# Down projection of a hybrid attention layer: ten and thirteen pairs by seven products, the first one's sums queued further on, the first half's closing additions in steps

## The chip, the cores and the metric

The kernel runs on one core of one Trainium2 chip. A core has several engines that each work through their own list of instructions in order and wait for one another by semaphores: TensorE (PE in the profile: matrix products; PEld is its loading of weights), VectorE (DVE), ScalarE (ACT), GpSimd (POOL) and SyncE (SP). SP, ACT and POOL also issue DMA transfers, each from a queue of its own (SPq, POOLq). The metric is device time in microseconds (us), the median of several runs.

## What is computed

One decoder layer on 256 positions with 2048 channels, in float32: a combined input projection, two kinds of attention side by side (8 heads each), an output projection, and an MLP of 8192 hidden channels. The change lies in the last step, the product of `u` (256 x 8192) with `w_down` (8192 x 2048) and the norm around it:

```python
x = x + _rmsnorm(mixed @ w_out[layer], norm_attn_post[layer])
h = _rmsnorm(x, norm_mlp_pre[layer])
u = jnp.square(jax.nn.relu(h @ w_up[layer]))
x = x + _rmsnorm(u @ w_down[layer], norm_mlp_post[layer])
```

## The kernel before

**Float32 by two parts.** Every operand of a product is split into two float32r parts: ACT copies it to `hi` (line 307) and DVE subtracts to get `lo` (line 308). A product is then three matmuls, hi·hi, hi·lo and lo·hi, all issued by the helper at line 297. The same is done for the weights, tile by tile, as they come from memory.

**The down projection** runs in two halves of the output's columns, c = 0 (columns 0 to 1023) and c = 1 (1024 to 2047). Each half sums over 64 chunks of 128 hidden channels, taken as 32 pairs. Four PSUM banks per half hold the result `y`: two blocks of positions (b) by two column groups of 512 (n). A pair is worked in one of two ways:

- As two single chunks ("k" steps): each chunk is one weight tile of 128 x 1024, multiplied into four banks by three matmuls each, 24 matmuls for the pair.
- By seven products ("w" step, a Strassen scheme): the pair and the two blocks of positions form a 2 x 2 by 2 x 2 block product, done with seven block products in place of eight. Seven times three is 21 matmuls. Four of the products go into banks `md1`, `md6`, `md7`, `md5`, apart from `y`. In exchange DVE has to form sums: of the weights (tiles `t` and `u`, in `st_down`, lines 360 to 365), giving four weight tiles to split in place of two (called b11, b, u, t below; b11 is half as wide), and of the activations (`four_sums`, lines 1028 to 1030, then split into the tile `s`). The tuple `DOWN_SEVEN` lists which pairs of each half go this way.

For pairs that are in both halves' lists (`SHARED`), the parts `s` formed in half 0 are stored to memory by `keep_s` (SP, line 1022) and fetched again in half 1 by `down_back` (POOL, line 407), so that half 1 doesn't form them anew. The lo parts of `u` are likewise stored and fetched (`ukeep`, lines 1018 and 1011), one for each group of two pairs.

**Closing a half.** When the last pair by seven products of a half is through, `close` (lines 1085 and 1088) combines the md banks into four correction tiles. When all pairs are through, half 0 is finished by `half_evac` (lines 1217 to 1227), while half 1 has begun: for each of its four banks DVE adds the correction to `y` (line 1223), ACT takes the sum of squares (`square`, line 1165), and DVE multiplies by the norm's gain (line 1227). The md banks of half 1 are the y banks of half 0, so half 1's first pair by seven products cannot start before `half_evac` has read them.

**The order of the work** is written by the program itself. All weight tiles of the program form one list (`weights.specs`). When PE is about to use tile i, `weights.get` emits the loads and splits up to tile i + 6 (`W_AHEAD`). The tiles lie in 8 slots (`W_BUFS`) and a slot is rewritten only when PE has used its tile; the loaded raw tiles lie in 5 (`RAW_BUFS`). `plan_seven` hangs the sums of a pair by seven products on a place in this list: `SUMS_AHEAD` = 2 tiles ahead of the pair's first tile, with the activations' sums two and one places before that. The load of the pair's weights goes on POOL's queue, into `ab_down` or, in turn, into `c` (half 0) or into `uT0` and `uT1` (half 1); as every engine's list is in order, POOL issues it as soon as the buffer's last readers are done. Chains such as `half_evac` are Python generators; each `yield` gives a time, in planned microseconds, after which the next piece is written into the engines' lists.

The tiles `s` have two buffers, `uhi`/`ulo` (the split `u` of a group of two pairs) also two.

Of the kernel before, what the change touches and what calls it, by code (L numbers as in the profile page):

```python
# [23 lines left out]
OP = mybir.AluOpType  # L24
# [5 lines left out]
NB = S // P  # L30
# [66 lines left out]
SUMS_AHEAD, LOAD_AHEAD = 2, 3  # L97
# [15 lines left out]
D_PREP = (50.0, 24.0, 12.0)  # L113


DOWN_SEVEN = ((7, 11, 13, 17, 19, 23, 25, 29), (4, 7, *range(9, 28, 2)))
SHARED = [k for k in DOWN_SEVEN[0] if k in DOWN_SEVEN[1]]
GT = FF // 512
DOWN_STEPS = [[s for kp in range(2 * GT)
# [145 lines left out]
def layer(nc, tc, io):  # L265
# [52 lines left out]
    weights = Weights(nc, wp, split, W_BUFS, W_AHEAD)  # L318
# [87 lines left out]
        st, left[c, kp] = down_parts(c, kp)  # L406
        nc.gpsimd.dma_start(out=st.bitcast(F32), in_=skeep[kp])

    def plan_seven(sums, fs, early, after, more=(), last=(), soon=False):

        at = max(len(weights.specs) - SUMS_AHEAD, after)
        if soon:
            more = (*more, (at - max(at - LOAD_AHEAD, after - 2), early))
        for n, f in (*more, (0, sums), *((0, f) for f in last)):
            weights.first.setdefault(at - n, []).append(f)
        return [weights.plan(f) for f in fs], len(weights.specs)
# [3 lines left out]
    wide_u, after, after_p = [], 0, 0  # L420
    for j in range(NUP):
        wide_u.append([])
        for what, k in UP_STEPS[j]:
            if what == "k":
                g = () if k in SCALED.get(j, ()) else (gcol[:, 8 + k:9 + k],)
                ts = [weights.plan(up_weight(j, k), 1, CW, *g)]
            elif what == "p":
# [3 lines left out]
                if j < 5:  # L431
                    at = max(len(weights.specs) - 2 * LOAD_AHEAD, after_p)
                    weights.first.setdefault(at, []).append(
                        lambda kept=kept: nc.gpsimd.dma_start(out=late["tu"], in_=kept))
                    ts = [weights.plan(src, 1, n) for src, n in srcs[:2]] + [weights.plan(
                        lambda hi, lo, o=o: split(hi, lo, late["tu"][:, o:o + CW])) for o in (CW, 0)]
                    after_p = len(weights.specs)
                else:
                    ts = [weights.plan(src, 1, n) for src, n in srcs]
            else:  # L440
                ts, after = plan_seven(*seven_up(j, k), after, soon=j < NUP - 1 or k == 0)
# [5 lines left out]
    def seven_down(c, kp):  # L447
        def load():

            n = DOWN_SEVEN[c].index(kp)  # L450
            raw = dpl["ab"]
            if n % 2:
                raw = [uT[i].rearrange("p k s -> p (k s)") for i in range(2)] if c else late["c"]
            return load_two(raw, nc.gpsimd, io["w_down"][2 * kp * P:(2 * kp + 2) * P, c * CW:(c + 1) * CW])

        return seven(load, lambda: [late["st"][:, i * CW:(i + 1) * CW] for i in range(2)])

    dpl, left, skeep, wide_d = {}, {}, {}, []
    for c in range(2):
        wide_d.append([])  # L460
        for what, k in DOWN_STEPS[c]:
            if what == "k":
                ts = [weights.plan(down_weight(c, k), 1, CW)]
            else:
                q, parts_q, back = [lambda c=c, k=k, f=f: f(c, k) for f in (down_sums, down_split, down_back)]
                more = ((), (back,)) if c and k in SHARED else (((2, q), (1, parts_q)),)
                ts, after = plan_seven(*seven_down(c, k), after, *more)
            wide_d[c].append((what, k, ts))

    def in_order(n, apart=(0, 0)):  # L470
# [392 lines left out]
    parts = [0] * NB  # L863
# [80 lines left out]
    for ns in ((0, 1), (2,), (3,)):  # L944
# [4 lines left out]
        for c, b, acc in proj(mixT, [ch_o[n] for n in ns], f"o{ns[0]}", order, heads_done):  # L949
            n = ns[c]  # L950
# [81 lines left out]
    sums = []  # L1032
# [130 lines left out]
    def square(n, b):  # L1163
        junk = dpl["dp"].tile([P, 512], BF16, tag="junk", bufs=1, name=f"junkd{n}{b}")
        nc.scalar.activation(junk, y[b][n], AF.Square, accum_out=ssd[b][:, n:n + 1])
# [51 lines left out]

    def half_evac(more, g_half):

        for n in range(2):  # L1220
            for b in range(NB):
                tt, out = nc.vector.tensor_tensor, more[b, n]
                tt(out=y[b][n], in0=y[b][n], in1=out, op=OP.add)
                yield 1.0
                square(n, b)
                yg[n, b] = out
                tt(out=out, in0=y[b][n], in1=g_half[n], op=OP.mult)
                yield 1.0

    def three_more(out, a, w):  # L1230

# [127 lines left out]
```

## Time and profile before

| what | before |
|---|---|
| three runs | 1047.55, 1047.61, 1047.78 us (median 1047.61) |
| the profiled execution | 1047.46 us, of which the span of the profile is 1045.7 us |
| TensorE clock granted, mean | 0.998 |
| PE busy | 1036.0 us, 4841 matmuls |
| DVE busy | 807.4 us, 1077 instructions |
| ACT busy | 636.5 us |
| DMA | 260.81 MB, mean 249 GB/s |
| the down projection, first matmul to end of the span | 700.89 to 1045.7 us |

How to read the rows that follow. A row of a group gives line, engine, operation, output tile <- inputs, shapes and count, then busy us in total and the mean in ns of one. A row of the timeline begins with start and duration in us, counted from the start of the span; in square brackets is the idle time just before it and what ended it. Consecutive instructions of an engine overlap a little: a DVE subtraction of 128 x 1024 lasts 1.22 us, yet the next one starts 1.14 us after it.

### The profile page before, as it was taken

Reading aid. Unit: us, or ns where it says so; the run is one execution under the profiler, and the core shown is the slowest. Engines: PE = TensorE matmul, PEld = TensorE weight load, DVE = VectorE, ACT = ScalarE, POOL = GpSimd, SP = SyncE. Lnnn points to the kernel's source line nnn. Section 1 sums busy time; section 2 is a strip of 40 time slices with the busy share of each in tenths; the row PEclk is TensorE's granted clock in tenths of the full one; section 3 lists DMA queues with packets and bytes.
Section 4 is the critical chain, followed back from the end, with each engine's and each line's share of the span. In section 5 each row is a group of like instructions: output and inputs, shape, how many; then the busy total and the mean of one; then the engine's idle time right before and its main releaser. Section 6 shows DMA issues by size and latency. Waiting matters only on the chain.

```text
span 1045.7 us, 13573 instructions
## 1 busy us (share of the span) xinstructions
PE 1036.0 (99%) x4841; PEld 862.9 (83%) x4841; DVE 807.4 (77%) x1077; ACT 636.5 (61%) x855; POOL 99.5 (10%) x157
## 2 busy tenths in 40 slices
PE   9999999999999999999999999999999999999996
PEld 6888889888888888888888888888888888888885
DVE  7666536567557659988889798887899988989995
ACT  7675436566545558666756766665666564766662
POOL 0011111112001000010100000000000001112100
PEclk9999999999999999999999999999999999999999
DMA  9999879699878296757766656468778767789952
GB/s 340 344 304 277 216 204 318 201 252 302 235 215 262 86 352 210 263 207 246 259 207 231 222 198 213 148 231 312 256 271 314 261 226 262 263 301 323 364 195 83
DMA packets 93141, 260.81 MB, mean 249 GB/s; under 512 B 8721, under 2 KB 12817, under 8 KB 91665
## 3 DMA queue, kind: packets, MB, share of 16 engines
q1 hardware_dynamic: 71056, 190.09, 52.6%
q0 software_dynamic: 21152, 68.69, 23.2%
q10 hardware_dynamic: 864, 1.16, 0.3%
q8 instruction: 38, 0.62, 0.2%
q14 instruction: 31, 0.25, 0.1%
HBM read 244.18 MB, written 39.32 MB: 271 GB/s over the span
## 4 chain that ended last, share of the span: by engine, by line
PE 98%; DMA 1%; DVE 0%; ACT 0%; SPq 0%; DVEq 0%; POOL 0%; issue 0%; ACTq 0%
PE y L297 26%; PE acc_u L297 25%; PE acc_o L297 8%; PE m L297 7%; PE md L297 5%; PE acc_v L297 4%; PE acc_qk L297 4%; PE acc_ckv L297 2%; PE acc_ukv L297 2%; PE acc_q L297 2%; PE acc_cq L297 2%; PE acc_k L297 2%; PE acc_uq L297 2%; PE rt L301 1%; PE y L1233 1%; PE sc_b L297 1%
## 5 line engine op out<-in xcount | busy, mean ns | idle before, releaser
L308 DVE TENSOR_TENSOR lo<-raw,hi 128x1024 fp32r<-128x1024 f32 (+3 forms) x240 | 269.2, 1139 | 95.1 <-ACT hi L307 94.2
L307 ACT ACTIVATE hi<-raw 128x1024 fp32r<-128x1024 f32 (+3 forms) x240 | 234.4, 990 | 96.6 <-DMA raw<-in_w_in 20.7
L297 PE MATMUL y<-hi,uhi 128*128 128x512 f32 x376 | 146.7, 390 | 0.0
L297 PE MATMUL y<-hi,ulo 128*128 128x512 f32 x376 | 146.3, 389 | 0.0
L297 PE MATMUL y<-lo,uhi 128*128 128x512 f32 x376 | 146.3, 389 | 0.0
L297 PE MATMUL acc_u<-hi,hT_hi 128*128 128x512 f32 x356 | 141.6, 398 | 0.0
L297 PE MATMUL acc_u<-hi,hT_lo 128*128 128x512 f32 x356 | 139.1, 391 | 0.0
L297 PE MATMUL acc_u<-lo,hT_hi 128*128 128x512 f32 x356 | 138.9, 390 | 0.0
L312 DVE SCALAR_TENSOR_TENSOR lo<-raw,gcol,hi 128x1024 fp32r<-128x1024 f32 x72 | 90.6, 1280 | 18.0 <-ACT hi L311 17.7
L311 ACT ACTIVATE hi<-raw,gcol 128x1024 fp32r<-128x1024 f32 x72 | 81.9, 1149 | 21.0 <-DMA raw<-in_w_up 12.9
L297 PEld LDWEIGHTS y<-hi,ulo 128*128 128x128 f32 x376 | 70.6, 188 | 14.7
L297 PEld LDWEIGHTS y<-hi,uhi 128*128 128x128 f32 x376 | 70.6, 188 | 14.6
L297 PEld LDWEIGHTS y<-lo,uhi 128*128 128x128 f32 x376 | 70.6, 188 | 14.4
L297 PEld LDWEIGHTS acc_u<-hi,hT_lo 128*128 128x128 f32 x356 | 66.8, 188 | 14.3 <-DVE hT_lo L308 0.2
L297 PEld LDWEIGHTS acc_u<-lo,hT_hi 128*128 128x128 f32 x356 | 67.0, 188 | 13.0
L297 PEld LDWEIGHTS acc_u<-hi,hT_hi 128*128 128x128 f32 x356 | 66.9, 188 | 12.8
L297 PE MATMUL m<-hi,st 128*128 128x512 f32 x156 | 56.5, 389 | 0.0
L297 PE MATMUL acc_o<-hi,mixT_hi 128*128 128x512 f32 x128 | 51.8, 405 | 0.0
L308 DVE TENSOR_TENSOR lo<-st_down,hi 128x1024 fp32r<-128x1024 f32 x40 | 48.0, 1220 | 4.2 <-ACT hi L307 4.2
L297 PE MATMUL acc_o<-hi,mixT_lo 128*128 128x512 f32 x128 | 50.2, 392 | 0.0
L297 PE MATMUL acc_o<-lo,mixT_hi 128*128 128x512 f32 x128 | 50.0, 390 | 0.0
L307 ACT ACTIVATE hi<-st_down 128x1024 fp32r<-128x1024 f32 x40 | 42.1, 1053 | 11.3 <-PE y L297 9.8
(341 smaller groups left out, 2040.6 us busy)
## 6 DMA issues: line engine op xcount, KB each, us to landing
raw<-in_w_down SPq DMA_DIRECT2D x88, 512.0 KB, 6.0
raw<-in_w_up SPq DMA_DIRECT2D x86, 512.0 KB, 4.5
raw<-in_w_in SPq DMA_DIRECT2D x55, 512.0 KB, 7.1
raw<-in_w_out SPq DMA_DIRECT2D x32, 512.0 KB, 8.1
ab<-in_w_up POOLq DMA_DIRECT2D x28, 512.0 KB, 5.0
sums<-in_w_up SPq DMA_DIRECT2D x20, 512.0 KB, 7.2
ab_down<-in_w_down POOLq DMA_DIRECT2D x20, 512.0 KB, 6.6
tu<-sums POOLq DMA_DIRECT2D x8, 1024.0 KB, 5.1
```

The source lines that it names most:

```text
L297: nc.tensor.matmul(out, a, b, start=start, stop=stop)
L301: nc.tensor.transpose(out, a, ident)
L307: nc.scalar.activation(hi, src, AF.Copy)
L308: nc.vector.tensor_tensor(out=lo, in0=src, in1=hi.bitcast(F32), op=OP.subtract)
L311: nc.scalar.activation(hi, src, AF.Copy, scale=g)
L312: nc.vector.scalar_tensor_tensor(out=lo, in0=src, scalar=g, in1=hi.bitcast(F32), op0=OP.mult, op1=OP.subtract)
L1233: nc.tensor.matmul(out, a[x], w[z], start=False, stop=(x, z) == (1, 0), skip_group_check=True)
```

## The change

The list of half 0 grows from eight to ten pairs (5 and 27 are new), that of half 1 from twelve to thirteen (3 and 5 for 4; the rest stays). The shared pairs are then nine in place of seven (5 and 27 are new). For the first pair of half 0 alone, `plan_seven` is called so that the sums stand directly ahead of the pair's first tile (`ahead=0`) in place of two tiles earlier, and its load is written into POOL's list two or three tiles ahead of them (`soon`). `half_evac` is rewritten as six steps 1.5 planned us apart, in which the addition of a bank, the square of the bank before it and the multiplication of the one before that are written together; before, it was eight steps of 1.0 with add and then square and multiply of one bank.

```diff
-DOWN_SEVEN = ((7, 11, 13, 17, 19, 23, 25, 29), (4, 7, *range(9, 28, 2)))
+DOWN_SEVEN = ((5, 7, 11, 13, 17, 19, 23, 25, 27, 29), tuple(range(3, 28, 2)))
...
-    def plan_seven(sums, fs, early, after, more=(), last=(), soon=False):
+    def plan_seven(sums, fs, early, after, more=(), last=(), soon=False, ahead=SUMS_AHEAD):
 
-        at = max(len(weights.specs) - SUMS_AHEAD, after)
+        at = max(len(weights.specs) - ahead, after)
...
-                more = ((), (back,)) if c and k in SHARED else (((2, q), (1, parts_q)),)
-                ts, after = plan_seven(*seven_down(c, k), after, *more)
+                more = ((), (back,)) if c and k in SHARED else (((2, q), (1, parts_q)), ())
+                first = (c, k) == (0, DOWN_SEVEN[0][0])
+                ts, after = plan_seven(*seven_down(c, k), after, *more, soon=first, ahead=0 if first else SUMS_AHEAD)
...
-        for n in range(2):
-            for b in range(NB):
-                tt, out = nc.vector.tensor_tensor, more[b, n]
-                tt(out=y[b][n], in0=y[b][n], in1=out, op=OP.add)
-                yield 1.0
-                square(n, b)
-                yg[n, b] = out
-                tt(out=out, in0=y[b][n], in1=g_half[n], op=OP.mult)
-                yield 1.0
+        parts, tt = [(n, b) for n in range(2) for b in range(NB)], nc.vector.tensor_tensor
+        for i in range(6):
+            if i > 1:
+                n, b = parts[i - 2]
+                yg[n, b] = more[b, n]
+                tt(out=yg[n, b], in0=y[b][n], in1=g_half[n], op=OP.mult)
+            if i < 4:
+                n, b = parts[i]
+                tt(out=y[b][n], in0=y[b][n], in1=more[b, n], op=OP.add)
+            if 0 < i < 5:
+                square(*parts[i - 1])
+            yield 1.5
```

The new lists change what stands where on the engines. Two places matter below. The first is DVE's list towards the end of half 0, from the second single chunk of pair 26. Before, pair 27 is two single chunks, and the sums and `s` of pair 29 come with them (`lo<-raw` is the split of a single chunk; `ulo` that of a group of activations):

```order
L308 TENSOR_TENSOR lo_7439<-raw_7436,hi_7438 128x1024
L1028 TENSOR_TENSOR st_down<-uT_6389 128x256
L1029 TENSOR_TENSOR st_down<-st_down,uT_6389 128x128
L1030 TENSOR_TENSOR st_down<-uT_6389,st_down 128x128
L308 TENSOR_TENSOR lo_7460<-raw_7457,hi_7459 128x1024
L308 TENSOR_TENSOR s_29_7466<-st_down,s_29_7466 128x512
L308 TENSOR_TENSOR lo_7472<-raw_7469,hi_7471 128x1024
L360 TENSOR_TENSOR st_down<-c 128x1024
L364 TENSOR_TENSOR st_down<-st_down,c 128x512
L365 TENSOR_TENSOR st_down<-st_down,c 128x512
L308 TENSOR_TENSOR lo_7489<-raw_7486,hi_7488 128x1024
```

With the change the same stretch, from the second single chunk of pair 26 to the first of pair 28, holds the four tiles of pair 27 as well:

```order
L308 TENSOR_TENSOR lo_7464<-raw_7461,hi_7463 128x1024
L308 TENSOR_TENSOR lo_7480<-ab_down,hi_7479 128x512
L308 TENSOR_TENSOR lo_7487<-ab_down,hi_7486 128x1024
L1029 TENSOR_TENSOR st_down<-uT_6391 128x256
L1030 TENSOR_TENSOR st_down<-st_down,uT_6391 128x128
L1031 TENSOR_TENSOR st_down<-uT_6391,st_down 128x128
L308 TENSOR_TENSOR lo_7500<-st_down,hi_7499 128x1024
L308 TENSOR_TENSOR s_29_7509<-st_down,s_29_7509 128x512
L308 TENSOR_TENSOR lo_7513<-st_down,hi_7512 128x1024
L360 TENSOR_TENSOR st_down<-c 128x1024
L364 TENSOR_TENSOR st_down<-st_down,c 128x512
L365 TENSOR_TENSOR st_down<-st_down,c 128x512
```

The three splits of single chunks have become one of a single chunk and four of pair 27 (the first of them half as wide).

The second place is DVE's list at the start of half 1, where `half_evac` stands between the splits of half 1's first pair by seven products. Before (lines 1223 and 1227 are the addition and the multiplication, `ab_down` and `st_down` the tiles of pair 4):

```order
L1223 TENSOR_TENSOR y_6346<-y_6346,c 128x512
L1227 TENSOR_TENSOR c<-y_6346,g_half_7170 128x512
L308 TENSOR_TENSOR lo_7798<-raw_7795,hi_7797 128x1024
L1223 TENSOR_TENSOR y_6348<-y_6348,c 128x512
L1227 TENSOR_TENSOR c<-y_6348,g_half_7170 128x512
L308 TENSOR_TENSOR lo_7818<-ab_down,hi_7817 128x512
L1223 TENSOR_TENSOR y_6347<-y_6347,c 128x512
L1227 TENSOR_TENSOR c<-y_6347,g_half_7171 128x512
L308 TENSOR_TENSOR lo_7838<-ab_down,hi_7837 128x1024
```

With the change (lines 1229 and 1226 are the addition and the multiplication, `ab_down` and `st_down` the tiles of pair 3, and the last rows the sums of pair 5):

```order
L1229 TENSOR_TENSOR y_6346<-y_6346,c 128x512
L1229 TENSOR_TENSOR y_6348<-y_6348,c 128x512
L308 TENSOR_TENSOR lo_7822<-ab_down,hi_7821 128x1024
L1226 TENSOR_TENSOR c<-y_6346,g_half_7184 128x512
L1229 TENSOR_TENSOR y_6347<-y_6347,c 128x512
L308 TENSOR_TENSOR lo_7842<-st_down,hi_7841 128x1024
L1226 TENSOR_TENSOR c<-y_6348,g_half_7184 128x512
L1229 TENSOR_TENSOR y_6349<-y_6349,c 128x512
L308 TENSOR_TENSOR lo_7862<-st_down,hi_7861 128x1024
L1226 TENSOR_TENSOR c<-y_6347,g_half_7185 128x512
L1226 TENSOR_TENSOR c<-y_6349,g_half_7185 128x512
L363 TENSOR_TENSOR st_down<-uT_3779 128x512
```

A multiplication no longer follows directly on the addition of its own bank, and the sums of a second pair (5) follow at once, where before four splits stood between.

## The prediction

> **What bounds the kernel now.** I read the page's first and fourth part, then PE's own waits, then the chain of work through the down projection, and last the timelines of DVE, ACT and POOL there.
>
> ```profile
> PE 1036.0 (99%) x4841; PEld 862.9 (83%) x4841; DVE 807.4 (77%) x1077; ACT 636.5 (61%) x855; POOL 99.5 (10%) x157
> PE 98%; DMA 1%; DVE 0%; ACT 0%; SPq 0%; DVEq 0%; POOL 0%; issue 0%; ACTq 0%
> ...
> PE warm L538 <- DVE zero L535: 1.2, 1, 1.2
> PE qrt L301 <- DVE qT L811: 0.2, 1, 0.2
> ```
>
> PE sets the end. The last two rows are all of PE's waits: in the down projection it never waits. So what the change can win is matmuls taken away, and what it can lose is a wait of PE where there is none now. In the chain, pairs of single chunks and pairs by seven products alternate in half 1:
>
> ```profile
> 860.71 32.64 PE y L297 x144
> ...
> 934.15 5.44 PE y L297 x24
> 944.35 5.44 PE y L297 x24
> ```
>
> A k pair is 24 matmuls in 5.44 us, 0.2267 us each; two pairs come every 10.20 us, which is 45 matmuls of 0.2267, so the 21 of a w pair take 4.76 us. One matmul takes no less in either kind. The first row holds pairs 30 and 31 of half 0 and 0 to 3 of half 1: pair 29 ends at 860.71 and half 1 begins at 871.59.
>
> **What is taken away.** Half 0 gains two w pairs, half 1 one: 3 pairs x 3 matmuls x 0.2267 = **2.04 us** of PE. No row shows PE idle there, so nothing beyond this can be won.
>
> **What is added, and who carries it.** DVE is the engine next to full:
>
> ```profile
> 970.00:985.00 15.00, 15.00 (x68) 12.40 (x67) 14.70 (x17) 10.87 (x12) 2.12 (x4) 1.00 1.01 392
> ...
> L308 DVE TENSOR_TENSOR lo<-raw,hi 128x1024 fp32r<-128x1024 f32 x88 | 105.0, 1219 | 13.7 <-ACT hi L307 13.7
> L360 DVE TENSOR_TENSOR st_down<-ab_down 128x1024 f32<-128x1024 f32 x10 | 12.2, 1223 | 0.8 <-DMA ab_down<-in_w_down 0.5
> L308 DVE TENSOR_TENSOR s<-st_down,s 128x512 fp32r<-128x512 f32 x13 | 8.9, 686 | 3.0 <-ACT s L307 3.0
> L365 DVE TENSOR_TENSOR st_down<-st_down,ab_down 128x512 f32<-128x512 f32 x10 | 6.9, 693 | 0.3
> L308 DVE TENSOR_TENSOR lo<-ab_down,hi 128x512 fp32r<-128x512 f32 x10 | 6.8, 682 | 0.0
> L1028 DVE TENSOR_TENSOR st_down<-uT 128x256 f32<-128x256 f32 x11 | 4.6, 416 | 0.0
> L1029 DVE TENSOR_TENSOR st_down<-st_down,uT 128x128 f32<-128x128 f32 x11 | 3.2, 292 | 0.4
> ```
>
> (In the stretch's row the columns after its length are PE, PEld, DVE, ACT, POOL, clock, DMA share, GB/s.) As single chunks a pair costs DVE two splits, 2.44 us. By seven products: sums 1.22 + 0.69 + 0.69 = 2.60 (line 364 is as long as 365), b11 0.68, three splits 3.66, in all 6.94; where its own `s` is formed, 0.42 + 0.29 + 0.29 for the small sums and 0.69 more, 8.63. Half 0: 2 x (8.63 - 2.44) = 12.4. Half 1: one pair more but one `s` fewer (3, 9, 15, 21 for 4, 9, 15, 21, 27): 6.94 - 2.44 - 1.69 = 2.8. Together 15.2 us more on DVE, in 335 us of down projection. The stretch quoted, 98% busy, is already one chunk pair and one w pair in turn, so DVE can keep up even there; what the 15.2 us cost is decided where the w pairs lie thickest, by how far DVE is ahead of PE. I call that distance the spare time: the moment PE wants a tile less the moment its `lo` is done.
>
> **Today's smallest spare time** comes in half 1 when a pair forms its own `s`: ACT may write that buffer only when PE has used the pair two w pairs earlier. For pair 15 that is pair 11, which ends where the chain shows 934.15:
>
> ```profile
> 934.18 0.63 ACT L307 ACTIVATE s<-st_down 128x512 fp32r<-128x512 f32 x1 [2.75 <-PE md L297]
> 934.85 0.69 DVE L308 TENSOR_TENSOR s<-st_down,s 128x512 fp32r<-128x512 f32 x1 [0.99 <-ACT s L307]
> 935.80 1.23 DVE L308 TENSOR_TENSOR lo<-st_down,hi 128x1024 fp32r<-128x1024 f32 x1 [0.26 <-ACT hi L307]
> ...
> 939.60 2.35 DVE L308 TENSOR_TENSOR lo<-raw,hi 128x1024 fp32r<-128x1024 f32 x2
> ```
>
> The first split of pair 14 is done at 939.60 + 1.22 = 940.82, 6.67 after pair 11's end. PE begins pair 14 at 944.35 and wants `lo` one matmul later, 944.58. Spare: 3.8 us.
>
> **Place one: pair 28 of half 0.** With 23, 25, 27 and 29 by seven products the same wait now comes in half 0: `s` of 27 waits for pair 23, `s` of 29 for pair 25. Let E be pair 23's end. As above, pair 26's first tile is done at E + 6.67 and wanted at E + 10.43. From there to pair 28's first tile DVE has, at the spacing of back-to-back rows (1.14 for a full split): `ulo` and the second chunk 2.3, b11 0.6, b, u and t 3.4, the small sums and `s` 1.7, the sums 2.6, the chunk itself 1.1: 11.7 us, while PE takes 10.2. Spare: 3.8 - 1.5 = **2.3 us**. After it there are no sums until half 1, and it recovers: pair 30 needs 4.6 of DVE for PE's 4.76, and every single chunk after that gives back up to 1.6.
>
> The wait has a second condition that half 0 alone has: `s` of 23 and of 25 must first have been stored by `keep_s`, a transfer in SP's queue. Today's store of pair 25 is issued late:
>
> ```profile
> 813.04 17.79 SPq L189 DMA_DIRECT2D raw<-in_w_down  x5
> 830.88 0.42 SPq L1022 DMA_DIRECT2D skeep<-s  x1
> ```
>
> It stands behind the raw loads of pairs 26 to 28, each of which waits for a buffer. With pairs 25 and 27 no longer loaded by SP, the store of 23 stands behind pair 24's loads only, whose buffers came free some 20 us before E, so it goes as soon as `s` of 23 is formed, some 12 us before E, and lands in time (3.8 to 8.8 us for the seven stores; row below). I cost it at nothing, with 0 and 10 us as the bounds.
>
> ```profile
> L1022 SPq DMA_DIRECT2D skeep<-s x7: 373/425/543, 735.7 to 830.9; - x7
> DMA to landing us min/median/max: 3.8/5.8/8.8
> ```
>
> **Place two: pair 4 of half 1.** Pair 29 now ends 1.36 us earlier (two w pairs), 859.35; half 1 begins at 870.23, pair 3 at 886.55, pair 4 at 891.31. DVE's queue, followed row by row from pair 28, is through with pair 0 of half 1 at about 861.3. Then: close 2.4, small sums 1.0, six splits of chunks and `ulo` (four chunks, one `ulo`, one `s` 0.65) 6.4, sums 2.6, b11 0.6: 874.3. Then the eight additions and multiplications:
>
> ```profile
> 874.40 0.69 DVE L1223 TENSOR_TENSOR y<-y,c 128x512 f32<-128x512 f32 x1
> 875.84 0.69 DVE L1227 TENSOR_TENSOR c<-y,g_half 128x512 f32<-128x512 f32 x1 [0.76 <-ACT junkd L1165]
> ...
> DVE c L1227 <- ACT junkd L1165: 3.2, 4, 0.8
> ```
>
> 8 x 0.61 = 4.9, three splits 3.4, the sums of pair 5 2.6, pair 4's first split 1.1: 886.3. The rows also show why the additions were a hindrance: each multiplication waits about 0.8 us for ACT's square, 3.2 in all. In steps another instruction stands between; between all of it gone and all of it kept the split is done at 886.3 to 889.5 and PE wants it at 891.5. Spare: **2.0 to 5.2 us**; I take 3. The md banks need the same multiplications, done by 885, and the first is written at 886.55.
>
> The sums of pair 5 also need a load into `uT1`, which waits for ACT's copy of it, and that stands behind the first square. Today that load comes later and is just in time (the last row is that of the loads into `ab_down`, of the same size and queue):
>
> ```profile
> 883.29 1.07 POOL L378 DMA_DIRECT2D uT<-in_w_down  x2
> ...
> DVE st_down L363 <- DMA uT<-in_w_down: 0.2, 1, 0.2
> ...
> uT<-in_w_down POOLq DMA_DIRECT2D x2, 512.0 KB, 5.7
> DMA to landing us min/median/max: 4.9/6.6/9.6
> ```
>
> With the first addition at 874.3, square and copy are done at 876.7, and the load lands 5.7 to 9.6 us after its issue, by 883 to 887; DVE comes to it at 883 to 886. At the worst the tile is done at 890, still in time. The Trainium skill, DMA: Bandwidth & Descriptors, section "Anatomy of one DMA", puts such a transfer at about 2.0 us plus bytes by 436 GB/s, for 524 KB an estimate of 3.2 us. The trace does not agree (4.9 at the least, beside other traffic); by that rule the load would be early and the sum would stay 2.04.
>
> **Place three: pair 6 of half 0.**
>
> ```profile
> 701.35 1.07 POOL L378 DMA_DIRECT2D ab_down<-in_w_down  x2 [57.82 <-PE acc_u L297]
> ...
> 718.75 1.22 DVE L360 TENSOR_TENSOR st_down<-ab_down 128x1024 f32<-128x1024 f32 x1
> ```
>
> Pair 5 begins ten chunks and 1.2 us of transposes after 700.89, at about 729.3. Today's first sums run at 718.75; with the sums directly ahead of b11 they come at about 717, and from there to pair 6's first tile there are 13 us of DVE (two sums 5.2, five full splits with `ulo` 5.7, b11, small sums and `s` 2.3): 730.1, wanted at 734.3. Spare: **4 us**. The load, issued when the up projection's last matmul frees the space, lands by 711 even with 9.6 us. That the sums stand later costs nothing here; placed earlier they would hold up chunks that PE wants first.
>
> In half 1 from pair 5 on, the alternation is today's, and pair 27, no longer forming its own `s`, is easier. ACT gains less than DVE and is at 10.9 of 15 where DVE is at 14.7. Two more stores and two more fetches of 0.5 MB are 2 MB in 90.
>
> **The sum.** 2.04 off the profiled execution's 1047.46 gives 1045.42; its time lies 0.15 under the median, so against the median of 1047.61 it is **1045.6**, 0.195% less. 0.2% is 2.1 us, about what a measurement of this kernel can tell from no change: the full gain ends just short of it.
>
> **The rivals.**
> 1. The full gain, no wait of PE: 1045.6. For it: the three spare times above are all positive, with bounds. Chance 0.68. The three runs before lie 0.23 us apart, and 0.05 us decides over the 0.2% line, so about a third of it falls beyond.
> 2. DVE late by little. Spare times of 2 to 3 us rest on sums of some 25 durations; 5% on 60 us of queue (from pair 23 to pair 4 of half 1) is 3 us. A wait of 0.3 to 2 us at pair 28 or at pair 4 gives 1045.9 to 1047.6. Against it: the durations scatter by 1% only. Chance 0.20.
> 3. The other side: the store of `s` holds up ACT. If the store of pair 23 is issued not before pair 24's splits but after them, as today's at 830.88, it lands 5.8 us later, ACT's `s` of 27 comes about 8 us late, and beyond the spare 3.8 PE waits, again at 29: two waits of about 4 us give 1045.6 + 8 = 1053.6. It decides from a landing later than E + 3.8. For it: SP's queue is today almost always waiting for buffers. Against: the queue's order, above. Chance 0.12.
> That the steps of `half_evac` do nothing is part of place two's bounds (3.2 us kept): spare still 2.0, time unchanged.
>
> The likeliest is the full gain. The range takes in rival 1 with its scatter and most of rival 2: 1045.3 to 1047.3. Faster by over 0.2%: 0.26 (a third of 0.68, and little else). Within: 0.62. Slower: 0.12.
>
> **What would show it.** Right: 9 fewer matmuls, PE still without a wait after the attention part, the last `y` matmuls 2.04 us earlier, DVE's busy time up by about 15 us, the multiplications' wait on `junkd` near zero, an ACT wait of `s` on PE also in half 0. Wrong: a wait of PE on `lo` at pair 28 or of half 1's pair 4, on md banks at pair 3, or of ACT's `s` on a store.

## The result and the profile after

| | before | after |
|---|---|---|
| median | 1047.59 us (20 runs, 1046.81 to 1048.94) | 1045.68 us (20 runs, 1045.09 to 1047.99) |
| profiled execution, its span | 1047.46, 1045.7 us | 1045.31, 1043.4 us |
| matmuls | 4841 | 4832 |
| down projection, first to last `y` matmul | 700.89 to 1037.12: 336.23 us | 700.82 to 1035.01: 334.19 us |

The ratio is 0.9981, with a 95% interval of 0.9974 to 0.9987: 0.19% less, just inside the 0.2% that I called no change (the interval reaches to both sides of that line), and 0.1 us from the forecast. The last line of the table is the sharper one: the down projection is shorter by 2.04 us, which is nine matmuls of 0.2267 us and nothing else. That length, and not the span, is used for the comparisons below, since in some executions PE waits up to 1 us at 9 us from the start, far ahead of anything that is changed. Two of the eleven runs of the kernel with nine matmuls out (1754 and 2129 us) were slow ones and are left out of its median below.

The first and the fourth part of the page, and then PE's own waits, of the kernel after:

```profile
PE 1033.9 (99%) x4832; PEld 862.2 (83%) x4832; DVE 820.7 (79%) x1096; ACT 640.3 (61%) x862; POOL 103.8 (10%) x165
PE 99%; DMA 0%; DVE 0%; ACT 0%; DVEq 0%; POOL 0%; issue 0%; ACTq 0%
...
PE warm L539 <- DVE zero L536: 1.2, 1, 1.2
PE qrt L301 <- DVE qT L812: 0.2, 1, 0.2
```

PE's two waits are those of before, both outside the down projection. DVE is busy 13.3 us longer (15.2 were forecast; I added durations, which overlap by some 0.08 us from one instruction to the next). The chain of work shows the new pairs; 27 is now worked in 21 matmuls, so single chunks stand alone at 26 and 28:

```profile
838.88 5.44 PE y L297 x24
849.08 5.44 PE y L297 x24
859.27 27.20 PE y L297 x120
891.24 5.44 PE y L297 x24
```

Place one, pair 28 of half 0, first in DVE's timeline, and then in PE's:

```profile
845.96 1.22 DVE L308 TENSOR_TENSOR lo<-raw,hi 128x1024 fp32r<-128x1024 f32 x1
847.09 1.22 DVE L308 TENSOR_TENSOR ulo<-uT,uhi 128x1024 fp32r<-128x1024 f32 x1
```

```profile
849.14 0.39 PE L297 MATMUL y<-lo,uhi 128*128 128x512 f32 x1
849.37 0.39 PE L297 MATMUL y<-hi,ulo 128*128 128x512 f32 x1
```

`lo` is done at 847.18 and used at 849.14: 2.0 us to spare, 2.3 forecast. But `ulo` is done at 848.31 and used at 849.37: only 1.1. PE uses the two 0.23 us apart, DVE needs 1.13 for the second. I had looked at the wrong tile; an experiment below shows that this one decides, and that its spare time is smaller still.

Place two, DVE at the start of half 1 (the additions, the split of pair 3 behind them, and the first split of pair 4):

```profile
874.69 1.29 DVE L1229 TENSOR_TENSOR y<-y,c 128x512 f32<-128x512 f32 x2
878.03 1.23 DVE L308 TENSOR_TENSOR lo<-ab_down,hi 128x1024 fp32r<-128x1024 f32 x1 [2.05 <-ACT hi L307]
...
887.57 2.35 DVE L308 TENSOR_TENSOR lo<-raw,hi 128x1024 fp32r<-128x1024 f32 x2
```

Pair 4's first split is done at 888.79, and its matmul starts at 891.30: 2.5 us to spare (3 taken, 2.0 to 5.2 given). No multiplication waits for a square any more; the one wait left here, 2.05 us, is for a `hi` tile that stands behind the first square on ACT.

Place three, DVE's first sums of half 0 and the first split of pair 6, which PE begins at 734.84 (the chain's row):

```profile
713.71 1.22 DVE L360 TENSOR_TENSOR st_down<-ab_down 128x1024 f32<-128x1024 f32 x1
...
725.74 1.22 DVE L308 TENSOR_TENSOR lo<-raw,hi 128x1024 fp32r<-128x1024 f32 x1
```

It is done at 726.96, some 8 us ahead.

The stores of `s` in SP's queue, the group of all nine, and then the rows of pairs 23, 25 and 27:

```profile
L1023 SPq DMA_DIRECT2D skeep<-s x9: 319/423/577, 712.3 to 830.1; - x9
...
DMA to landing us min/median/max: 3.5/6.8/8.4
```

```profile
803.47 0.33 SPq L1023 DMA_DIRECT2D skeep<-s  x1
...
815.73 0.32 SPq L1023 DMA_DIRECT2D skeep<-s  x1
...
830.10 0.32 SPq L1023 DMA_DIRECT2D skeep<-s  x1
```

These three are issued as soon as `s` is formed, not behind the next loads. The store that mattered for place one is that of pair 23, whose buffer `s` of 27 takes: it is issued 25 us before pair 23's end (12 forecast). ACT's waits of `s` for PE are now 11.2 us in four, where they were 8.2 in three (`ACT s L307 <- PE md L297`); the new one is that of pair 27.

### The profile page after: what moved, and what is told of

It is laid out like the page before. It is cut to its first block, busy times and chain, and to the rows that moved or that the text cites. A ratio compares the mean times of both kernels' runs of the same rounds, so it can differ in the third digit from the quotient of the medians.

```text
span 1043.4 us, 13587 instructions
## 1 busy us (share of the span) xinstructions
PE 1033.9 (99%) x4832; PEld 862.2 (83%) x4832; DVE 820.7 (79%) x1096; ACT 640.3 (61%) x862; POOL 103.8 (10%) x165
## 4 chain that ended last, share of the span: by engine, by line
PE 99%; DMA 0%; DVE 0%; ACT 0%; DVEq 0%; POOL 0%; issue 0%; ACTq 0%
PE acc_u L297 25%; PE y L297 25%; PE acc_o L297 8%; PE m L297 7%; PE md L297 6%; PE acc_qk L297 4%; PE acc_v L297 4%; PE acc_ckv L297 2%; PE acc_ukv L297 2%; PE acc_q L297 2%; PE acc_cq L297 2%; PE acc_k L297 2%; PE acc_uq L297 2%; PE rt L301 1%; PE y L1237 1%; PE sc_b L297 1%
## 5 line engine op out<-in xcount | busy, mean ns | idle before, releaser
L308 DVE TENSOR_TENSOR lo<-raw,hi 128x1024 fp32r<-128x1024 f32 (+3 forms) x234 | 262.0, 1137 | 86.6 <-ACT hi L307 85.5
L307 ACT ACTIVATE hi<-raw 128x1024 fp32r<-128x1024 f32 (+3 forms) x234 | 228.2, 988 | 83.9 <-DMA raw<-in_w_in 16.0
L297 PE MATMUL acc_u<-hi,hT_hi 128*128 128x512 f32 x356 | 141.8, 398 | 0.0
L297 PE MATMUL y<-hi,uhi 128*128 128x512 f32 x358 | 139.8, 391 | 0.0
L297 PE MATMUL y<-hi,ulo 128*128 128x512 f32 x358 | 139.5, 390 | 0.0
L297 PE MATMUL y<-lo,uhi 128*128 128x512 f32 x358 | 139.5, 390 | 0.0
L297 PE MATMUL acc_u<-hi,hT_lo 128*128 128x512 f32 x356 | 139.3, 391 | 0.0
L297 PE MATMUL acc_u<-lo,hT_hi 128*128 128x512 f32 x356 | 139.0, 391 | 0.0
L311 ACT ACTIVATE hi<-raw,gcol 128x1024 fp32r<-128x1024 f32 x72 | 81.9, 1149 | 20.9 <-DMA raw<-in_w_up 12.9
L297 PEld LDWEIGHTS y<-hi,ulo 128*128 128x128 f32 x358 | 67.2, 188 | 14.1
L297 PEld LDWEIGHTS y<-lo,uhi 128*128 128x128 f32 x358 | 67.3, 188 | 13.8
L297 PEld LDWEIGHTS acc_u<-hi,hT_lo 128*128 128x128 f32 x356 | 66.8, 188 | 14.3 <-DVE hT_lo L308 0.2
L297 PEld LDWEIGHTS y<-hi,uhi 128*128 128x128 f32 x358 | 67.2, 188 | 13.7
L297 PEld LDWEIGHTS acc_u<-lo,hT_hi 128*128 128x128 f32 x356 | 67.0, 188 | 13.0
L297 PEld LDWEIGHTS acc_u<-hi,hT_hi 128*128 128x128 f32 x356 | 67.0, 188 | 12.8
L297 PE MATMUL m<-hi,st 128*128 128x512 f32 x156 | 56.5, 390 | 0.0
L308 DVE TENSOR_TENSOR lo<-st_down,hi 128x1024 fp32r<-128x1024 f32 x46 | 55.1, 1219 | 0.8 <-ACT hi L307 0.8
L297 PE MATMUL acc_o<-hi,mixT_hi 128*128 128x512 f32 x128 | 51.9, 405 | 0.0
L307 ACT ACTIVATE hi<-st_down 128x1024 fp32r<-128x1024 f32 x46 | 48.2, 1051 | 5.7 <-PE y L297 5.1
L297 PE MATMUL acc_o<-hi,mixT_lo 128*128 128x512 f32 x128 | 50.2, 393 | 0.0
L297 PE MATMUL acc_o<-lo,mixT_hi 128*128 128x512 f32 x128 | 50.0, 391 | 0.0
```

The source lines that it names most:

```text
L297: nc.tensor.matmul(out, a, b, start=start, stop=stop)
L307: nc.scalar.activation(hi, src, AF.Copy)
L308: nc.vector.tensor_tensor(out=lo, in0=src, in1=hi.bitcast(F32), op=OP.subtract)
L311: nc.scalar.activation(hi, src, AF.Copy, scale=g)
```

## The experiments

"Down" is the length of the down projection as above, in the profiled execution; the last column is the sum of PE's idle times that the timeline shows there. Each kernel was timed beside the kernel before on the same chip (1047.8 to 1047.9 us there).

| run | down, us | median, us | ratio, 95% interval | PE waits in it, us |
|---|---|---|---|---|
| before | 336.23 | 1047.59 | 1 | 0 |
| after | 334.19 | 1045.68 | 0.9981, 0.9974 to 0.9987 | 0 |
| nine matmuls out | 334.19 | 1045.99 | 0.9980, 0.9971 to 0.9989 | 0 |
| new steps alone | 336.23 | 1047.46 | 0.9998, 0.9990 to 1.0007 | 0 |
| old closing | 335.33 | 1047.09 | 0.9995, 0.9986 to 1.0003 | 0.80 |
| old closing, square last | 338.17 | 1048.61 | 1.0008, 0.9999 to 1.0017 | 1.63 |
| first sums earlier | 334.74 | 1046.48 | 0.9986, 0.9977 to 0.9995 | 0.33 |
| sum of pair 29, twice more | 334.77 | 1046.63 | 0.9987, 0.9978 to 0.9996 | 0.29 |
| ... four times more | 336.22 | 1047.72 | 1.0000, 0.9992 to 1.0009 | 1.47 |
| ... seven times more | 340.01 | 1051.3 | 1.0035, 1.0022 to 1.0048 | 3.63 |
| eleven pairs, five in a row | 334.21 | 1045.88 | 0.9983, 0.9974 to 0.9992 | 0.39 |
| eleven pairs, 4 + 4 + 3 | 334.64 | 1046.38 | 0.9987, 0.9978 to 0.9996 | 0.74 |
| eleven pairs, 4 + 3 + 4 | 333.51 | 1045.05 | 0.9978, 0.9969 to 0.9987 | 0 |
| all thirteen pairs | 346.94 | 1057.45 | 1.0090, 1.0076 to 1.0103 | 9.7 |

**Is the gain the matmuls alone?** The kernel before, with nine matmuls left out and nothing added: the three products of the last bank (b = 1, n = 1) of chunks 11 and 55 of half 0 and of chunk 7 of half 1, so that these nine products are missing from `y`.

```diff
-                    down_mm(c, u, k, b, n, w, t == 0, t == len(wide_d[c]) - 1)
+                    if (c, k, b, n) not in ((0, 11, 1, 1), (0, 55, 1, 1), (1, 7, 1, 1)):
+                        down_mm(c, u, k, b, n, w, t == 0, t == len(wide_d[c]) - 1)
```

> The kernel before with nine matmuls of the down projection left out (three each for the last bank of chunks 11 and 55 of half 0 and of chunk 7 of half 1, so the result lacks these terms) and nothing else changed. Theory: nine matmuls of 0.2267 us are 2.04 us, and the change's added work on DVE, ACT and the queues costs nothing: the last matmul 2.04 us earlier than before, time 1045.6, the same as the change within 0.4. Rival: the added work costs something that PE's waits do not show; then this kernel is faster than the change by that, 0.5 to 1.5 us.

The down projection takes 334.19 us, to the hundredth what it takes after the change. So the sums, splits and transfers that the change adds cost nothing, and the matmuls are the whole gain. The page's first row shows DVE where it was before the change:

```profile
PE 1033.4 (99%) x4832; PEld 861.1 (83%) x4832; DVE 807.0 (77%) x1077; ACT 636.4 (61%) x855; POOL 99.5 (10%) x157
```

**The steps of the closing, alone and left out.** First the kernel before with `half_evac` in the new six steps and nothing else changed (the diff is the last piece of the one above).

> The kernel before with half_evac in the six new steps and nothing else changed (the old lists of pairs). The theory: in the kernel before TensorE waits nowhere in the down projection, so that work done earlier there gives nothing back: VectorE's waits on junkd go, the down projection stays at 336.2 us, the time at that of the kernel before (ratio 1.000, within 0.001). The rival, that the shorter closing is itself worth something, gives 0.3 us or more off the down projection and a ratio under 0.999.

336.23 us, ratio 0.9998: nothing is gained. But DVE is earlier. The splits of pair 5, the first single chunks behind the closing, in the kernel before (both chunks in one row) and then the first of them in this one:

```profile
890.68 2.35 DVE L308 TENSOR_TENSOR lo<-raw,hi 128x1024 fp32r<-128x1024 f32 x2
```

```profile
886.83 1.22 DVE L308 TENSOR_TENSOR lo<-raw,hi 128x1024 fp32r<-128x1024 f32 x1
```

Before, the first was done at 891.90, and PE's matmul with it starts at 898.17: 6.3 us to spare. The steps make that 10.2. With the old lists the closing was thus not a tight place at all, and what the steps save there is of no use.

Then the changed kernel with the old closing:

```diff
-        parts, tt = [(n, b) for n in range(2) for b in range(NB)], nc.vector.tensor_tensor
-        for i in range(6):
...
+        for n in range(2):
+            for b in range(NB):
+                tt, out = nc.vector.tensor_tensor, more[b, n]
+                tt(out=y[b][n], in0=y[b][n], in1=out, op=OP.add)
+                yield 1.0
+                square(n, b)
+                yg[n, b] = out
+                tt(out=out, in0=y[b][n], in1=g_half[n], op=OP.mult)
+                yield 1.0
```

> The change with the closing additions of half 0 put back as they were (add, square, multiply, bank by bank). My theory: the gain is the nine matmuls alone and the steps only add to the spare time. DVE loses up to 3.2 us to ACT's squares in place of the 2.05 us it now waits there, so the spare time of pair 4 in half 1 falls from 2.7 to about 1.5 us, PE waits nowhere, and the time is that of the change, 1045.7 (within 0.5). Rival: the steps are what makes three more pairs possible; then PE waits 0.5 to 2 us for a split of pair 4 or for the md banks of pair 3, and the time is 1046.2 to 1047.7.

Here the steps are worth 1.14 us. PE's timeline at pair 4 of half 1, and then DVE's ahead of it:

```profile
893.48 0.50 PE L297 MATMUL y<-lo,uhi 128*128 128x512 f32 x1 [0.80 <-DVE lo L308]
```

```profile
877.34 0.69 DVE L1228 TENSOR_TENSOR c<-y,g_half 128x512 f32<-128x512 f32 x1 [0.76 <-ACT junkd L1166]
879.23 1.23 DVE L308 TENSOR_TENSOR lo<-ab_down,hi 128x1024 fp32r<-128x1024 f32 x1 [1.20 <-ACT hi L307]
...
882.83 1.23 DVE L308 TENSOR_TENSOR lo<-st_down,hi 128x1024 fp32r<-128x1024 f32 x1 [0.26 <-ACT hi L307]
```

I had counted the four waits for squares (3.2 us). Between them the splits wait too, for `hi` tiles that ACT could form only after the square: 1.20, 0.26 and 0.25. That makes 4.9 us where the new steps have 2.05, and each stop also loses the overlap with the instruction before. From the first addition to pair 4's first split DVE takes 16.3 us here (875.89 to 892.21) and 12.9 with the steps (874.69 to 887.57): 3.4 more, where 2.5 are to spare.

**What makes the engines take turns?** The old closing again, with two lines in the other order:

```diff
-                square(n, b)
                 yg[n, b] = out
                 tt(out=out, in0=y[b][n], in1=g_half[n], op=OP.mult)
+                square(n, b)
```

> The changed kernel with half_evac in its old eight pieces, and in them the square of a bank written behind the multiplication and not ahead of it; the result is the same. With the old pieces as they were, TensorE waited 0.8 us at pair 4 of half 1, VectorE having waited 0.8 us for each of four squares and 0.25 to 1.2 us for each hi tile behind a square. The theory, that the multiplication waits for the square only because it is written behind it: the waits on junkd go (3.2 us), while those on hi stay or grow by up to 0.7 each, since ScalarE's square and so its hi come no earlier; pair 4 is then done 0.5 to 3 us earlier, TensorE doesn't wait there (spare -0.3 to 2.2 us) and the down projection takes 334.2 to 334.6 us. The rival, that the two engines go in turn whatever the order (the square then waits for the multiplication, and hi for the square): the wait at pair 4 stays at 0.5 us or more, down projection 335.0 us or more.

The rival was right, and more than right: the multiplication no longer waits for the square, but the square for the multiplication, and with it the `hi` behind the square. One turn on ACT, and one on DVE behind it:

```profile
881.07 0.60 ACT L1166 ACTIVATE junkd<-y 128x512 bf16<-128x512 f32 x1 [2.69 <-DVE c L1227]
```

```profile
882.73 1.23 DVE L308 TENSOR_TENSOR lo<-st_down,hi 128x1024 fp32r<-128x1024 f32 x1 [1.76 <-ACT hi L307]
```

In this turn DVE waits 1.76 us in one stop, where the old order had 0.81 and 0.26 in two; from the first addition to pair 4's first split it takes 17.7 us (16.3 in the old order). Whichever of square and multiplication is written second waits for the first, though both only read the bank; and a `hi` behind a late square makes the next split late. The order of the change takes this out by putting work of another bank between the two. Why an engine waits for another that only reads the same bank, these runs don't show.

**Place one, and its spare time.** The changed kernel, in which the last sum of the weights of pair 29, just ahead of pair 28's first split, is done 2, 4 or 7 times more (the result is the same):

```diff
-            tt(out=u[:, H:], in0=u[:, :H], in1=b[:, :H], op=OP.add)
+            for _ in range(1 + again):
+                tt(out=u[:, H:], in0=u[:, :H], in1=b[:, :H], op=OP.add)
...
-        return seven(load, lambda: [late["st"][:, i * CW:(i + 1) * CW] for i in range(2)])
+        sums, fs, early = seven(load, lambda: [late["st"][:, i * CW:(i + 1) * CW] for i in range(2)])
+        return ((lambda: sums(2)) if (c, kp) == (0, 29) else sums), fs, early
```

> The changed kernel, in which VectorE does the last sum of the weights of pair 29 of half 0 two times more (1.3 us more just ahead of pair 28's first split; the result is the same). The theory says that this place has 2.1 us to spare: 1.3 us more leaves 0.8, so TensorE doesn't wait at pair 28, the down projection keeps 334.2 us and the time is that of the changed kernel, 1045.7 us. The rival, that the spare time is less than the rows of the trace say (a wait from 0.3 us up at pair 28), gives 1046.0 to 1047.0 us and a row of TensorE waiting for lo at about 852.

The theory missed. `lo` was in time, as it said, but behind it `ulo` was not; DVE's row, and then PE's:

```profile
849.54 1.22 DVE L308 TENSOR_TENSOR ulo<-uT,uhi 128x1024 fp32r<-128x1024 f32 x1
```

```profile
850.81 0.50 PE L297 MATMUL y<-hi,ulo 128*128 128x512 f32 x1 [0.29 <-DVE ulo L308]
```

Relative to PE the tiles are 1.45 us later than in the changed kernel: the 2.0 us of `lo` hold, the 1.1 us of `ulo` don't. The down projection is 0.58 us longer, twice the idle time in brackets. The wait is longer in the row of the weight load, in which PE takes in `ulo`:

```profile
850.81 0.19 PEld L297 LDWEIGHTS y<-hi,ulo 128*128 128x128 f32 x1 [0.72 <-DVE ulo L308]
```

Where nothing waits, this load stands one matmul ahead of the one that uses it: in the changed kernel at the moment at which the matmul with `lo` starts:

```profile
849.14 0.19 PEld L297 LDWEIGHTS y<-hi,ulo 128*128 128x128 f32 x1
```

Counted to there, `ulo` has 0.8 us to spare and not 1.1.

> The changed kernel with the last sum of the weights of pair 29 done four times more by VectorE (2.9 us more ahead of pair 28's first split; two times more gave a wait of 0.3 us on ulo, seven times more waits of 3.0 and 0.6 us and, after them, 3.5 us of half the granted clock). Theory one, that a wait costs its length and some 0.3 us for starting again, and that the clock falls only after a wait of about 3 us: waits of 1.9 us together at pair 28, the down projection 336.2 to 336.5 us, the granted clock 1.00 right behind. Theory two, that any wait of over 1 us lowers the clock for 3.5 us: 1.7 us more, 337.9 to 338.2 us, and rows of matmuls about 0.43 us apart behind the wait.

Theory one. Both tiles are waited for, and the down projection is 2.03 us longer, 0.28 us for each of the two waits beyond the 1.47 shown. PE's rows, and the stretch behind them (columns: PE, PEld, DVE, ACT, POOL, clock, DMA share, GB/s), in which the granted clock stays at 1.00:

```profile
850.46 0.49 PE L297 MATMUL y<-lo,uhi 128*128 128x512 f32 x1 [0.83 <-DVE lo L308]
851.59 0.50 PE L297 MATMUL y<-hi,ulo 128*128 128x512 f32 x1 [0.64 <-DVE ulo L308]
```

```profile
852.00:854.00 2.00, 2.00 (x11) 1.63 (x10) 2.00 (x3) 2.00 (x3) 0.00 (x0) 1.00 0.69 223
```

> The change with the last of pair 29's weight sums in half 0 done eight times in place of once (same values), which makes DVE 7 x 0.61 to 0.72 = 4.3 to 5.0 us later at pair 28's first chunk. Theory: the spare time there is 2.1 us, so PE waits 2.1 to 2.9 us at pair 28 and nowhere else (afterwards the wait itself is spare time): 1047.8 to 1048.6, the gain gone. Rival: there is more cover than the one row shows (other slots, PE taking another tile first): PE waits less than 1 us, 1045.7 to 1046.7.

The place is the right one, but the loss of 5.82 us is far over the expected length of the wait. PE's rows, and the stretches behind:

```profile
852.29 0.50 PE L297 MATMUL y<-lo,uhi 128*128 128x512 f32 x1 [3.00 <-DVE lo L308]
853.42 0.50 PE L297 MATMUL y<-hi,ulo 128*128 128x512 f32 x1 [0.63 <-DVE ulo L308]
```

```profile
854.00:856.00 2.00, 2.00 (x7) 1.63 (x6) 2.00 (x3) 2.00 (x3) 0.00 (x0) 0.62 0.67 227
856.00:858.00 2.00, 2.00 (x6) 1.52 (x6) 2.00 (x3) 0.84 (x2) 0.00 (x0) 0.53 0.66 215
858.00:860.00 2.00, 2.00 (x11) 1.62 (x10) 2.00 (x3) 0.28 (x1) 0.00 (x0) 1.00 0.03 12
```

After the wait the clock is halved: from 854.45 to 858.09 nine matmuls take 3.64 us where they would take 2.04. These 1.6 us, the 3.63 in brackets and 0.3 for each of the two starts make 5.8.

**Where the first sums stand.** The changed kernel, with the first pair's sums two tiles ahead like all others, and its load not brought forward:

```diff
-                ts, after = plan_seven(*seven_down(c, k), after, *more, soon=first, ahead=0 if first else SUMS_AHEAD)
+                ts, after = plan_seven(*seven_down(c, k), after, *more)
```

> The change with the first pair's sums where they were (two tiles ahead of its first tile, load not brought forward in POOL's list). Theory: PE wants the chunks behind them only 10 us later, so even a DVE that waits for the load (issued about 701.4, landed by 708 to 712) does not reach PE: no wait of PE, 1045.7 (within 0.5), DVE waiting 0 to 4 us on the load. Rival: the sums hold up the chunks of pairs 3 and 4 and PE waits 1 to 3 us there: 1046.7 to 1048.7.

The down projection is 0.55 us longer, between the two theories and by neither's way: no chunk waits. ACT's rows, and then PE's:

```profile
705.51 0.63 ACT L307 ACTIVATE s<-st_down 128x512 fp32r<-128x512 f32 x1 [0.54 <-DVE st_down L1031]
...
707.47 0.68 ACT L983 ACTIVATE r<-acc_u,rstd_pre 128x512 f32<-128x512 f32 x1
```

```profile
708.20 0.66 PE L301 MATMUL rt<-ident,r 128*128 128x128 f32 x4 [0.33 <-ACT r L983]
```

With the sums go the small sums and `s` of the pair. ACT, which has to empty the last banks of the up projection (`r`, which PE then transposes), waits 0.54 us for the small sums, comes to `r` late, and PE waits 0.33 us for it.

**How many pairs can half 0 take?** Three kernels that differ from the changed one in the list of half 0 only:

```diff
-DOWN_SEVEN = ((5, 7, 11, 13, 17, 19, 23, 25, 27, 29), tuple(range(3, 28, 2)))
+DOWN_SEVEN = ((5, 7, 9, 11, 13, 17, 19, 23, 25, 27, 29), tuple(range(3, 28, 2)))
...
+DOWN_SEVEN = ((5, 7, 9, 11, 15, 17, 19, 21, 25, 27, 29), tuple(range(3, 28, 2)))
...
+DOWN_SEVEN = (tuple(range(5, 30, 2)), tuple(range(3, 28, 2)))
```

> The changed kernel with pair 9 by seven products in half 0 too (5, 7, 9, 11, 13 in a row, eleven pairs). Three matmuls less are 0.68 us. The theory: in a row of pairs taken in turn VectorE loses 1.5 us against TensorE in each period of 10.2 us, from a spare time of 3.8 us: 3.8 at pair 8, 2.3 at pair 10, 0.8 at pair 12; nothing waits, the down projection takes 333.5 us, the time is 1045.0 us. The rival: the loss of a period is larger than 1.5 (2 us already give -0.2 at pair 12), TensorE waits some tenths at pair 12, and with them the gain is spent: 1045.5 to 1046.5 us.

Five in a row: 334.21, the gain of 0.68 us is spent, as the rival said. Not by a much larger loss in each period, however (`lo` has 3.5, 2.0 and 0.4 us to spare at pairs 8, 10 and 12, some 1.6 less each time), but again at `ulo`, at pair 12:

```profile
767.44 0.50 PE L297 MATMUL y<-hi,ulo 128*128 128x512 f32 x1 [0.39 <-DVE ulo L308]
```

> The changed kernel with eleven pairs by seven products in half 0 in rows of four, three and three or four: 5, 7, 9, 11, then 15, 17, 19, 21, then 25, 27, 29. The theory: after three periods in a row the spare time is 3.8 - 1.5 = 2.3 us, as at pair 28 of the changed kernel, and two pairs of single chunks in between give it back; TensorE waits nowhere, the down projection takes 333.5 us (three matmuls less, 0.68 us), the time is 1045.0 us. The rival is that a row beginning anew (15, 25) has no time to recover: waits of 0.5 to 2 us at pairs 18, 20 or 28, and 1045.5 to 1047.0 us.

Rows of four, four and three: no tile of DVE is late, but a transfer is, in half 1 at pair 20. PE's row, and then POOL's issues ahead of it:

```profile
973.64 0.50 PE L297 MATMUL y<-hi,ulo 128*128 128x512 f32 x1 [0.74 <-DMA ulo<-ukeep]
```

```profile
962.55 0.54 POOL L407 DMA_DIRECT2D s<-skeep  x1 [8.07 <-PE md L297]
963.08 0.54 POOL L1012 DMA_DIRECT2D ulo<-ukeep  x1
```

With 21 a shared pair, the fetch of its `s` stands ahead of that of `ulo` in POOL's queue and waits for PE. `ulo` is fetched at 963.08 and lands 10.5 us later; in the changed kernel the same fetch is issued at 961.57 and lands 7.3 us later. So the queue's order makes it 1.5 us later, and a slower transfer another 3.2. Why the transfer is slower this run doesn't show; in the next kernel but one, where pair 21 is not shared, both are gone.

> The changed kernel with every odd pair from 5 to 29 by seven products in half 0, thirteen as in half 1. Nine matmuls less than in the changed kernel, 2.04 us: without a wait 1043.6 us, which is what the rival says (VectorE is busy 79% over the whole, and in half 1 the same alternation runs without a wait). The theory: where half 0 also has to form and store s, VectorE needs 11.7 us for each period of 10.2. The spare time of 3.8 us at pair 8 is used up by pair 14; from there TensorE waits up to 1.5 us in each of eight periods, 8 to 12 us in all: down projection 340 to 344 us, 1051 to 1056 us, with waits for lo at the first chunk behind each pair by seven products. If such waits lower the granted clock, as after the wait of 3 us in the run with a delayed sum, it is more.

All thirteen: the theory's side, and beyond its range, because the waits begin at pair 12 and not at 14, each costs more than its idle time (last section), and one of 1.27 us comes in half 1, for a fetched `ulo`. PE's timeline, one row of each of two periods:

```profile
777.25 0.49 PE L297 MATMUL y<-lo,uhi 128*128 128x512 f32 x1 [0.37 <-DVE lo L308]
...
789.02 0.49 PE L297 MATMUL y<-lo,uhi 128*128 128x512 f32 x1 [0.37 <-DVE lo L308]
```

The periods are 11.77 us long. Here DVE sets the pace (it is busy for 29.59 of the 30 us from 800 to 830), and this is a direct measurement of the 11.7 us that the prediction added up from durations.

**Eleven pairs without pair 21.** Eleven pairs in rows of four, three and four, so that pair 21 isn't shared:

```diff
+DOWN_SEVEN = ((5, 7, 9, 11, 15, 17, 19, 23, 25, 27, 29), tuple(range(3, 28, 2)))
```

> The changed kernel with eleven pairs by seven products in half 0 in rows of four, three and four: 5, 7, 9, 11, then 15, 17, 19, then 23, 25, 27, 29. With 15, 17, 19, 21 in a row TensorE waited 0.7 us in half 1 for a fetched ulo, which stood in GpSimd's queue behind the fetch of s for pair 21; here pair 21 is not shared, and the row that is new in half 0 has four pairs only. The theory: no place has less to spare than pair 28 of the changed kernel (1.1 us at ulo), TensorE waits nowhere in the down projection, which takes 333.5 us (0.68 less); 1045.0 us in the median. The rival: the fetch is late for another reason (the traffic of that stretch), a wait of 0.3 to 0.8 us appears in half 1 at pair 20 or at pair 10, and the down projection stays at 334.0 us or more.

333.51 us, as the theory had it: three matmuls less, and PE waits nowhere in the down projection. The page's first row and PE's waits:

```profile
PE 1033.3 (99%) x4829; PEld 860.7 (83%) x4829; DVE 824.5 (79%) x1101; ACT 639.3 (61%) x864; POOL 105.5 (10%) x168
...
PE warm L539 <- DVE zero L536: 1.2, 1, 1.2
PE acc_qk L297 <- ACT hi L307: 0.3, 1, 0.3
PE qrt L301 <- DVE qT L812: 0.2, 1, 0.2
```

Its median is 1045.05 us, its ratio to the kernel before 0.9978 (0.9969 to 0.9987). Against the changed kernel the 0.68 us show in the trace; the times alone can't tell the two apart.

## Why the prediction was right, and where not

- **The gain is the matmuls: right.** 2.04 us forecast, 2.04 measured; the run with nine matmuls left out gives the same, so the added work is hidden, as I costed it. On which side of the 0.2% line the time falls is chance: the forecast lay 0.05 us from it.
- **Place one: right in its sum, wrong in its tile.** The period of 11.7 us is 11.77 where it can be measured, and `lo` had 2.0 us for 2.3 forecast (0.17 of the difference is that I took the start of the pair from the chain's row, which starts a little into the pair). But the spare time was counted to `lo` alone. `ulo` is DVE's next tile and is used one matmul later, so it has 0.9 less: 1.1 us, and 0.8 counted to its weight load. The forecast held by that much, and as far as `ulo` goes by luck.
- **Today's smallest spare time: right, a little too large.** Counted from the rows of the matmuls, `lo` of pair 14 had 3.6 us (3.8 forecast). No `lo` of a weight tile in the kernel before had less than the 3.5 of pair 20 (done at 971.47, used at 975.01). For `ulo` I gave none.
- **Place two: right in its number, wrong in its bound.** 2.5 us measured for 3 taken. The lower bound rested on keeping 3.2 us of waits on squares; with the old closing the stretch is 3.4 us longer than with the new, its waits are 4.9 us, and the spare time falls to -0.9. "That the steps of `half_evac` do nothing" and "spare still 2.0, time unchanged" therefore failed: without them 1.14 us are lost. The step that failed is that I let only the multiplications wait, and not the splits behind the squares' `hi`. On the old lists the steps do give nothing, as the run with the steps alone shows.
- **Place three: mis-sized to the safe side.** Pair 6's first split is done at 726.96 and its chain row starts at 734.84: about 8 us, 4 forecast, since the sums ran at 713.71 and not at 717. "Placed earlier they would hold up chunks" had the direction right (0.55 us lost) and the mechanism wrong: what is held up is ACT's emptying of the up projection.
- **The load into `uT1`** was issued at 877.35, forecast 876.7, and DVE didn't wait for it at 885.04.
- **Rival 2, DVE late by little,** did not happen. With 1.1 us in hand at place one (0.8 to the weight load) it was closer than the spare times of 2 to 4 us suggested: 1.45 us of more work there bring it about.
- **Rival 3, the store of `s`,** did not happen; the order of SP's queue, which I gave against it, is what the rows show (803.47 for pair 23, 815.73 for 25).

## What to carry to other kernels

When the bound engine never waits, price added work on its neighbours by the spare time of each tile where that work lies thickest, and count it for every tile that the next product needs, not for the first: the second tile comes a whole instruction later and is wanted no more than one matmul later. Look for pairs of engines that take turns on the same buffer; such a chain of short waits costs more than the wait that the profile names, and work of another buffer put in between removes it. A saving there is worth nothing by itself and becomes worth its time once the list is denser (here 0 and 1.14 us), so try such edits together.

## What the runs showed of the hardware that I had not expected

**A wait costs more than its idle time.** A short wait of PE takes about 0.3 us beyond what the timeline shows as idle: 0.29 shown and 0.58 lost, 0.39 and 0.70, 0.80 and 1.14, 1.47 (two waits) and 2.03; with all thirteen pairs 9.7 (eighteen waits) and 14.8 (against 332.15 us, nine matmuls under the changed kernel). The starts of the matmuls show where it goes. Without a wait a matmul's row lasts 0.39 us but the next starts after 0.23, so the row ahead covers 0.16 of a wait; and behind the one that waited the next starts after 0.34 (850.13, 850.81, 851.15 and 851.38 in the run with two sums more).

**The clock after a wait.** After idle times of 3.00 and 0.63 us the granted clock was halved for some 3.6 us, with matmuls 0.43 us apart in place of 0.2267. In the run with the square last, three waits of 0.22, 0.92 and 0.49 us within 3.3 us were enough:

```profile
892.34 0.50 PE L297 MATMUL y<-hi,uhi 128*128 128x512 f32 x1 [0.92 <-ACT uhi L1011]
893.34 0.79 PE L297 MATMUL y<-lo,uhi 128*128 128x512 f32 x1 [0.49 <-DVE lo L308]
```

```profile
894.00:896.00 2.00, 2.00 (x6) 1.58 (x5) 2.00 (x3) 2.00 (x3) 0.54 (x1) 0.50 0.95 369
```

There 3.98 us were lost for 1.63 shown. Two waits of together 1.47 us within 2.1 us left the clock at 1.00. The Trainium skill, TensorE: Matmul & The Clock Gate, Part 1, section "What's actually happening", describes a gate that halves the clock after an idle window of about 3.4 us, a window that runs freely and isn't started by the work. The halved rate and its length of about one window agree with the trace. Read as a window that is idle from end to end, it does not agree: the longest single idle time in the run with the square last was 0.92 us. What share of it decides stays open; between 1.47 and 1.63 us of shown idle time, in one run each, is too little to place it.
